# Making the summed weights of layer 1's Strassen-like units in DRAM, ahead of their use

## The chip, the cores and the metric

The kernel runs on one core of a Trainium2 chip. The metric is the device time of one execution in microseconds (us), lower is better. A measurement is a set of runs; the middle one counts.

## What is computed

Two decoder layers on one sequence of 512 tokens and 1024 channels, all in float32. Layer 0 is a Conformer convolution module followed by a SwiGLU FFN, layer 1 is windowed attention over a shared key and value followed by a SwiGLU FFN, and a final RMSNorm closes. The change concerns the FFN of layer 1:

```
def swiglu_ffn(x, w_up, w_down):
    gate, up = jnp.split(x @ w_up, 2, axis=-1)
    return (jax.nn.silu(gate) * up) @ w_down
...
        h = h + swiglu_ffn(rmsnorm(h, norm_ffn[l]), ffn_w_up[l], ffn_w_down[l])
```

Here `w_up` is 1024 x 5632 and `w_down` is 2816 x 1024.

## The kernel before

**Chunks.** All weights lie in one DRAM tensor `W` as chunks of 128 x 1024 floats (512 KB). `PLAN` lists the chunks in the order in which TensorE uses them. For every chunk `advance()` is called once, as its matmuls are about to be written. It calls `load(u)`, which keeps the loads ahead of the use, and then splits up to three chunks ahead (L275): ScalarE (ACT) casts the raw chunk to the high part `whi` (L272), VectorE (DVE) subtracts to get the low part `wlo` (L275). Each product is then three matmuls, high x high, high x low, low x high (L354 to L356 in `mm3`, L846 for layer 1's down projection). There are four buffers each for `raw`, `whi` and `wlo`.

**The engines' queues.** Each engine works through its instructions in order. SyncE (SP) issues the plain loads. GpSimd (POOL) issues the adding DMAs, and a DMA that has to wait keeps what stands behind it on POOL waiting too. Plain and adding DMAs are queues q1 and q0 of the profile; both run on the same 16 DMA engines.

**Order of the work.** Convolution; layer 0's FFN in two parts, `HALVES0`: pairs 0 to 4 (once for each half of the tokens), then pairs 5 to 10 for all tokens, the "second part" (`ffn_part(0, 1, ...)`, 24 up chunks and 12 down chunks); key and value (4 chunks); queries (8 chunks) with attention interleaved; output projection (8 chunks); then layer 1's FFN by `STEPS1`, and the output.

**Layer 1's units.** Six of eleven up pairs (`SEVENS`) and five steps of the down projection (`low`) are done with seven products in place of eight, in the manner of Strassen and Winograd: 11 units of seven chunks each. Four of a unit's seven weight blocks are not plain blocks but sums, with the blocks A11 to A22 of the weight matrix:

```
SUMS = {"S1": ("A21", "A22"), "S2": ("A11", "S1"), "S3": ("A21", "A11"), "S4": ("A12", "S2")}
```

The signs are in the right-hand blocks, so that all four are additions. S2 needs S1, and S4 needs S2.

**How a sum is made before.** `load(u)` has three loops. The first runs up to nine chunks ahead and loads a sum's first block from `W` into a `sum` tile in SBUF (four buffers, L252, SP). The second loads plain chunks into `raw`, up to six ahead (L258, SP). The third, up to six ahead, issues the adding DMA for the second block (L264, POOL): from `W` for S1 and S3, from the `sum` tile of S1 or S2 for S2 and S4. Nothing of this begins before attention's buffers are given back, since the tiles come from a pool that is opened then. There are 44 sums: 44 loads of first blocks and 44 adds, 22 from `W` and 22 from another `sum` tile.

**Others that the prediction names.** In layer 0's second part `evac` multiplies gate and up on POOL (L642), and ACT splits the product (L516). In attention POOL scales the probabilities (L1320) ahead of the transposes on TensorE. In layer 1 a unit's evacuation combines the seven products on DVE and POOL (L789 to L806, with L792 on POOL and L798 on DVE), L820 makes the sums of the right-hand side, and L764 evacuates a plain pair; L855 and L853 add the down projection into the residual.

Of the kernel before, what the change touches and what calls it, by code (L numbers as in the profile page):

```python
# [11 lines left out]
F32 = mybir.dt.float32  # L12
F32R = mybir.dt.float32r
AF = mybir.ActivationFunctionType
ALU = mybir.AluOpType
# [3 lines left out]
P = 128  # L19
D = 1024  # L20
S = 512
# [54 lines left out]
SUMS = {"S1": ("A21", "A22"), "S2": ("A11", "S1"), "S3": ("A21", "A11"), "S4": ("A12", "S2")}  # L76
# [6 lines left out]
def is_block(c):  # L83
    return isinstance(c[2], str) if len(c) == 3 else False


def chunk_plan():
    plan = []

    def pw2():  # L90
        for g in range(2):
            for kp in range(KT // 2):
                plan.append(("pw2", kp, g))

    def ffn(layer, lo, hi):
        for pair in range(lo, hi):
            plan.extend(ups(layer, pair))
        for g in range(2):
            for kp in range(lo, hi):
                plan.append(("down", layer, kp, g))  # L100

    for _ in range(2):
        pw2()
        ffn(0, *HALVES0[0])
    ffn(0, *HALVES0[1])
    for part in range(2):
        for half in range(2):
            plan.append(("kv", part, half))
    for quarter in range(4):
        for half in range(2):  # L110
            plan.append(("q", half, quarter))
    for part in range(2):
        for g in range(2):
            for kp in range(2):
                plan.append(("o", part * 2 + kp, g))
    for kind, pair in STEPS1:
        plan.extend(blocks_of(kind, pair) if kind == "low" or by_seven(1, pair) else ups(1, pair))
    for g in range(2):
        plan.append(("down", 1, LAST, g))
    return plan  # L120


PLAN = chunk_plan()
# [5 lines left out]
CHUNK_AT = {c: i for i, c in enumerate(CHUNKS)}  # L129
# [70 lines left out]
def hybrid_trunk(ctx: ExitStack, tc: tile.TileContext, xT, W, prm_in, wdw_in, sinks, relb, onehot, fin, lead, out):  # L200
    nc = tc.nc
    cpool = ctx.enter_context(tc.tile_pool(name="const", bufs=1))
    quads = ctx.enter_context(tc.tile_pool(name="quads", bufs=11))
    wpool = ctx.enter_context(tc.tile_pool(name="wts", bufs=4))
# [3 lines left out]
    dpool = ctx.enter_context(tc.tile_pool(name="dram", bufs=1, space=DRAM))  # L208
# [3 lines left out]
    def uid(s):  # L212
        ctr[0] += 1
        return f"{s}{ctr[0]}"
# [4 lines left out]
    def quad(dt=F32R):  # L219
        return quads.tile([P, 4, 512], dt, tag="quad", name=uid("quad"))  # L220
# [6 lines left out]

    stream = {"dma": 0, "split": 0, "use": 0}
    raws, splits = {}, {}
    DMA_AHEAD, SUM_AHEAD, SPLIT_AHEAD = 6, 6, 3  # L230
    BASE_AHEAD = 9
    stream.update(base=0, sum=0)
    lo_engine = [nc.vector]
    biased = [None]
    sums_pool = [None]
    latest = []
    sums = {}

    def is_sum(c):
        return is_block(c) and c[2][0] == "S"  # L240

    def chunk(c, name=None):
        return W[CHUNK_AT[c if name is None else c[:2] + (name,)]]

    def load(u):
        while stream["base"] < min(len(PLAN), u + BASE_AHEAD):
            c = PLAN[stream["base"]]
            if is_sum(c):
                if sums_pool[0] is None:
                    break  # L250
                sums[c[2]] = raws[stream["base"]] = t = sums_pool[0].tile([P, 1024], F32, tag="sum", name=uid("sum"), bufs=4)
                nc.sync.dma_start(t, chunk(c, SUMS[c[2]][0]))  # L252
            stream["base"] += 1
        while stream["dma"] < min(len(PLAN), u + DMA_AHEAD):
            i = stream["dma"]
            if not is_sum(PLAN[i]):
                raws[i] = r = wpool.tile([P, 1024], F32, tag="raw", name=uid("raw"), bufs=4)
                nc.sync.dma_start(r, chunk(PLAN[i]))  # L258
            stream["dma"] += 1
        while stream["sum"] < min(stream["base"], u + SUM_AHEAD):  # L260
            c = PLAN[stream["sum"]]
            if is_sum(c):
                add = SUMS[c[2]][1]
                nc.gpsimd.dma_start(raws[stream["sum"]], made[c[:2] + (add,)] if add[0] == "S" else chunk(c, add),  # L264
                                    accum_op=ALU.add)
                made[c] = raws[stream["sum"]]
            stream["sum"] += 1

    made = {}

    def split_weights(hi, lo, src):
        on_act = nc.scalar.copy(hi, src).ins  # L272

        with tc.issue_after(biased[0]) if biased[0] else nullcontext():
            latest[:] = [on_act, lo_engine[0].tensor_sub(lo, src, f32(hi)).ins]  # L275

    def advance():
        u = stream["use"]
        load(u)
        while stream["split"] < min(len(PLAN), u + SPLIT_AHEAD):  # L280
            i = stream["split"]
            stream["split"] += 1
            if i in NATIVE:
                splits[i] = (raws.pop(i), None)
                continue
            hi = wpool.tile([P, 1024], F32R, tag="whi", name=uid("whi"))
            lo = wpool.tile([P, 1024], F32R, tag="wlo", name=uid("wlo"))
            splits[i] = (hi, lo)
            split_weights(hi, lo, raws.pop(i))
# [418 lines left out]
    class Rows:  # L708
# [12 lines left out]
        def sums(self):  # L721
            f = [quad(F32) for _ in range(2)]
            for i in range(KT):
                nc.scalar.mul(f[i // 4][:, i % 4, :], h[i], col(self.gain, i))
            b11, b12, b21, b22 = (x[:, :, s] for x in f for s in HALF)
            t1 = self.pool.tile([P, 1024], F32, tag="sum", name=uid("t1"), bufs=4).rearrange("p (k s) -> p k s", k=4)

            for name, t, f, a, b in (("T1", t1, nc.gpsimd.tensor_sub, b11, b12), ("T3", b12, nc.gpsimd.tensor_sub, b22, b12),
                                     ("T2", b11, nc.gpsimd.tensor_add, b12, b11), ("T4", b21, nc.gpsimd.tensor_sub, b11, b21)):
                f(t, a, b)  # L730
                yield
                both = quads.tile([P, 2, 4, 256], F32R, tag="quad", name=uid("rows"))
                self.block[name] = [both[:, a] for a in range(2)]
                split(self.block[name], t, name == "T2")
# [129 lines left out]
    raw = [x[:, HALF[1]] for x in xg]  # L864
# [13 lines left out]
    with tc.tile_pool(name="conv", bufs=2) as cv:  # L878
# [299 lines left out]
        base = seen[0]  # L1178
# [22 lines left out]
    base = seen[0]  # L1201
# [12 lines left out]
    nxt = Next(("kv", "mix1"))  # L1214


    if True:
        ffn_part(0, 1, x0["ffn0"], ALL, Both(), nxt.on_h)
        x, rms = nxt.x, nxt.rms
# [153 lines left out]
        def step():  # L1373
            next(pipe, None)
# [5 lines left out]
        for part in range(2):  # L1380
            for g in range(2):
                def heads_of(kt):
                    return tuple(os_[part, kt // 2][:, 2 * a + kt % 2, :] for a in range(2))

                if part == 0:

                    ws = [get("o", kp, g) for kp in range(2)]
                    banks = {}
                    for m0, kp in ((0, 0), (0, 1), (2, 0), (2, 1)) if g else ((0, 0), (2, 0), (0, 1), (2, 1)):
                        order = [(k, m) for k in range(2) for m in (m0, m0 + 1)]  # L1390
                        if kp:
                            order = [(k, m) for m in (m0, m0 + 1) for k in range(2)]
                        for k, m in order:
                            if m not in banks:
                                banks[m] = bank()
                            mm3(banks[m], [w[:, k, m * P:(m + 1) * P] for w in ws[kp]], heads_of(2 * kp + k),
                                kp == 0 and k == 0, kp == 1 and k == 1)
                            if kp and k:
                                nc.vector.tensor_add(h[g * 4 + m], banks[m], h[g * 4 + m])
                        if (g, m0, kp) in ((0, 0, 1), (1, 0, 0), (1, 2, 0), (1, 2, 1)):  # L1400
                            step()
                    continue
                banks = [bank() for _ in range(4)]
                down_group([(("o", part * 2 + kp, g), 2 * kp) for kp in range(2)], heads_of, banks)
                for m in range(4):
                    i = g * 4 + m
                    nc.vector.tensor_add(h[i], banks[m], h[i])
                    nxt.on_h(i)
            if part == 0:
                drain(pipe)  # L1410
                attn.close()
                seven = ExitStack()
                pool7 = sums_pool[0] = seven.enter_context(tc.tile_pool(name="seven", bufs=2))
                nxt = Rows("ffn1", pool7)

    flips = iter([(t, g) for t in range(NBLK) for g in range(2)])
# [9 lines left out]
    for kind, pair in STEPS1:  # L1426
# [6 lines left out]
        if by_seven(1, pair):  # L1433
            c = seven_pair(pair, nxt, pool7, flip if pair == SEVENS[0] else None)
        else:
            c = plain_pair(pair, nxt, pool7)
# [68 lines left out]
```

## Time and profile before

| | us |
|---|---|
| median of 3 runs | 1078.13 |
| lowest, highest run | 1073.57, 1079.31 |
| the profiled execution, its own time | 1076.19 |
| its span, first to last instruction | 1074.4 |

| engine | busy, share of the span |
|---|---|
| TensorE (PE) | 98% |
| VectorE (DVE) | 70% |
| ScalarE (ACT) | 51% |
| GpSimd (POOL) | 40% |

A busy time counts an instruction from start to end. Matmuls overlap, so a busy TensorE is not one at its peak; what can be read is where it is idle. A row of a timeline gives start and duration in us, the engine, the line and the tiles, and in brackets the idle time before it and what ended it. A row of a waits view gives the sum of such waits in us, their number and the longest. In the DMA view a queue has its packets, the MB moved, and the share of the stretch in which its packets kept the 16 DMA engines.

### The profile page before, as it was taken

What the parts mean: (1) busy time and instruction counts of PE and PEld (TensorE: products, weight loads), DVE (VectorE), ACT (ScalarE), POOL (GpSimd) and SP (SyncE); (2) the same over time, 40 slices, a digit from 0 to 9 for tenths busy, and PEclk for the clock granted to TensorE, in tenths of its full rate; (3) what the DMA queues carried; (4) which work ended last, traced back from release to release, by engine and by line L of the source; (5) the groups of instructions that cost most, each with busy time, mean ns of one, the idle gap of its engine ahead of it and who ended that gap; (6) DMA issues with size and microseconds to landing.
All of it is one profiled execution on the core that took longest, in us unless ns stands there. A gap on an engine that the chain in (4) does not pass through costs nothing.

```text
span 1074.4 us, 15965 instructions
## 1 busy us (share of the span) xinstructions
PE 1054.1 (98%) x5878; PEld 914.7 (85%) x5878; DVE 752.3 (70%) x1159; ACT 551.8 (51%) x968; POOL 428.6 (40%) x523
## 2 busy tenths in 40 slices
PE   9999999999999999999999999999999998999996
PEld 7888889999988888888888777788889897798885
DVE  3999987977777644434546566578776867859687
ACT  3887887765565333322343565475543444443453
POOL 3999997710321211111111354116433416425331
PEclk9999999999999999999999999999999999999998
DMA  9238045565565432223323211375689698888932
GB/s 353 87 97 98 3 153 201 176 227 187 177 186 186 158 98 98 99 98 98 97 79 99 79 59 60 126 187 129 186 213 240 193 275 226 235 211 244 242 99 79
DMA packets 50651, 164.86 MB, mean 153 GB/s; under 512 B 5483, under 2 KB 11788, under 8 KB 50572
## 3 DMA queue, kind: packets, MB, share of 16 engines
q1 hardware_dynamic: 43516, 139.67, 40.2%
q0 software_dynamic: 6336, 23.07, 11.6%
q10 hardware_dynamic: 720, 1.10, 0.3%
q8 instruction: 46, 0.75, 0.3%
q14 instruction: 33, 0.27, 0.1%
HBM read 147.04 MB, written 5.24 MB: 142 GB/s over the span
## 4 chain that ended last, share of the span: by engine, by line
PE 86%; DMA 6%; DVE 5%; issue 2%; POOL 1%; ACT 0%; SPq 0%; POOLq 0%; DVEq 0%; ACTq 0%
PE bank L354 18%; PE bank L356 18%; PE bank L355 17%; PE bank L904 10%; PE bank L386 5%; PE bank L846 5%; PE bank L352 4%; DMA sum<-sum 4%; PE bank L387 3%; DMA sum<-in_W_dram 2%; DVE wlo L275 2%; PE bank L1301 1%; PE bank L1343 1%; PE bank L1330 1%; DVE h L855 1%
## 5 line engine op out<-in xcount | busy, mean ns | idle before, releaser
L356 PE MATMUL bank<-quad,wlo 128*128 128x512 f32 (+1 forms) x1008 | 348.7, 346 | 2.2 <-DVE wlo L275 2.2
L354 PE MATMUL bank<-quad,whi 128*128 128x512 f32 (+1 forms) x1008 | 349.1, 347 | 0.0
L355 PE MATMUL bank<-quad,whi 128*128 128x512 f32 (+1 forms) x1008 | 348.7, 346 | 0.0
L275 DVE TENSOR_TENSOR wlo<-raw,whi 128x1024 fp32r<-128x1024 f32 x175 | 241.8, 1383 | 151.3 <-ACT whi L272 150.7
L272 ACT CAST whi<-raw 128x1024 fp32r<-128x1024 f32 x175 | 183.2, 1048 | 217.3 <-PE bank L355 144.3
L356 PEld LDWEIGHTS bank<-quad,wlo 128*128 128x128 f32 x1008 | 190.9, 189 | 26.2 <-DVE wlo L275 2.6
L354 PEld LDWEIGHTS bank<-quad,whi 128*128 128x128 f32 x1008 | 190.9, 189 | 24.5 <-issue 1.6
L355 PEld LDWEIGHTS bank<-quad,whi 128*128 128x128 f32 x1008 | 190.9, 189 | 23.2 <-issue 0.2
L946 POOL TENSOR_TENSOR pr<-pr,pr 128x256 f32<-128x256 f32 x208 | 156.5, 785 | 8.0 <-ACT pr L945 7.9
L953 DVE SCALAR_TENSOR_TENSOR bank<-apad,wdw,bank 128x256 f32<-128x256 f32 x248 | 112.4, 484 | 3.4
L945 ACT ACTIVATE pr<-apad,wdw 128x256 f32<-128x256 f32 x208 | 98.4, 501 | 15.0 <-POOL pr L946 13.2
L904 PE MATMUL bank<-quad,w 128*128 128x256 f32 x448 | 98.7, 380 | 0.0
L904 PEld LDWEIGHTS bank<-quad,w 128*128 128x128 f32 x448 | 84.9, 190 | 11.8 <-issue 0.2
L275 DVE TENSOR_TENSOR wlo<-sum,whi 128x1024 fp32r<-128x1024 f32 x44 | 64.0, 1455 | 18.3 <-ACT whi L272 18.1
L272 ACT CAST whi<-sum 128x1024 fp32r<-128x1024 f32 x44 | 46.0, 1047 | 58.9 <-PE bank L355 18.9
L465 POOL TENSOR_TENSOR tmp<-tmp,tmp 128x256 f32<-128x256 f32 (+1 forms) x28 | 26.7, 955 | 123.3 <-ACT tmp L461 86.6
L386 PE MATMUL bank<-quad,whi 128*128 128x512 f32 x212 | 75.9, 398 | 0.0
L264 POOL DMA_DIRECT2D sum<-sum x22 | 19.3, 875 | 120.1 <-DMA sum<-in_W_dram 45.0
L642 POOL TENSOR_TENSOR tmp<-tmp,tmp 128x512 f32<-128x512 f32 x12 | 17.2, 1433 | 112.0 <-DVE tmp L641 112.0
L387 PE MATMUL bank<-quad,wlo 128*128 128x256 f32 x212 | 59.3, 280 | 0.0
L356 PE MATMUL bank<-rows,wlo 128*128 128x256 f32 x192 | 54.4, 284 | 3.5 <-DVE wlo L275 3.5
L846 PE MATMUL bank<-wlo,fhi 128*128 128x512 f32 x140 | 55.3, 395 | 1.9 <-DVE wlo L275 1.9
(222 smaller groups left out, 1703.5 us busy)
## 6 DMA issues: line engine op xcount, KB each, us to landing
raw<-in_W_dram SPq DMA_DIRECT2D x187, 512.0 KB, 3.8
sum<-in_W_dram SPq DMA_DIRECT2D x44, 512.0 KB, 5.4
sum<-in_W_dram POOLq DMA_DIRECT2D x22, 512.0 KB, 7.4
sum<-sum POOLq DMA_DIRECT2D x22, 512.0 KB, 7.1
w<-in_W_dram SPq DMA_DIRECT2D x14, 512.0 KB, 8.7
fd<-fs SPq DMA_DIRECT2D x1, 3072.0 KB, 34.3
h<-in_xT_dram SPq DMA_DIRECT2D x8, 256.0 KB, 8.4
bias<-fd SPq DMA_DIRECT2D x8, 256.0 KB, 5.1
```

The source lines that it names most:

```text
L272: on_act = nc.scalar.copy(hi, src).ins
L275: latest[:] = [on_act, lo_engine[0].tensor_sub(lo, src, f32(hi)).ins]
L354: nc.tensor.matmul(out, w[0], x[0], start=start, stop=False)
L355: nc.tensor.matmul(out, w[0], x[1], start=False, stop=False)
L356: nc.tensor.matmul(out, w[1], x[0], start=False, stop=stop)
L386: nc.tensor.matmul(first[2], first[0], first[1], start=start, stop=False)
L387: nc.tensor.matmul(second[2], second[0], second[1], start=False, stop=stop)
L846: nc.tensor.matmul(out, x, w[:, ws], start=first and e == 0 and i == 0, stop=e == 1 and i == 2, skip_group_check=True)
L904: mm = nc.tensor.matmul(self.pb[:, w * W2:(w + 1) * W2], w1_of(ct, w, k), x[k] if x else xg[k][:, tok], start=k == 0, stop=k == KT - 1)
L945: on_act = nc.scalar.mul(pr, a[:, j:j + W2], tap(j))
L946: on_pool = nc.gpsimd.tensor_add(pr, acc, pr)
L953: on_dve = nc.vector.scalar_tensor_tensor(yt if i == nd - 1 else c, src, tap(i), c if i else self.shift, op0=ALU.mult, op1=ALU.add)
```

## The change

The sums are no longer made in SBUF as they are needed. `prepare()` is a generator that is started ahead of layer 0's second part and moved on by one step in every call of `advance()`, ahead of the loads. A step issues, for one sum, a copy of its first block from `W` to a DRAM tile of its own (SP), and three steps later the adding DMA onto that tile (POOL), whose source is `W` for S1 and S3 and the DRAM tile of S1 or S2 for S2 and S4. The order of the sums puts S4 of the unit before between S1 and S2, and the adds take 47 steps: the second part's 36 chunks, key and value, and seven chunks of the queries. In layer 1 a sum is then loaded like any chunk, into one of the four `raw` buffers, six ahead. The `sum` tiles in SBUF and `load`'s first and third loop go; a scratch tile (`t1`) that shared their buffers keeps one. The adding DMA now bears a cap of 4096 bytes on a contiguous piece; the copy has none. What is computed is the same.

```
+    def load(upto):
+        while stream["dma"] < min(len(PLAN), upto):
             i = stream["dma"]
-            if not is_sum(PLAN[i]):
-                raws[i] = r = wpool.tile([P, 1024], F32, tag="raw", name=uid("raw"), bufs=4)
-                nc.sync.dma_start(r, chunk(PLAN[i]))
+            r = wpool.tile([P, 1024], F32, tag="raw", name=uid("raw"), bufs=4)
+            nc.sync.dma_start(r, chunk(PLAN[i]))
+            raws[i] = r
             stream["dma"] += 1
-        while stream["sum"] < min(stream["base"], u + SUM_AHEAD):
...
+    def prepare():
+
+        units = [c[:2] for c in PLAN if is_block(c) and c[2] == "S1"]
+        adds, todo, before = [], [], None
+        for u in units:
+            adds += [u + ("S1",), *([before + ("S4",)] if before else []), u + ("S2",), u + ("S3",)]
+            before = u
+        adds.append(before + ("S4",))
+        for c in adds + [None] * 3:
+            if c is not None:
+                summed[c] = dpool.tile([P, 1024], F32, tag=uid("sum"), name=uid("sum"))
+                nc.sync.dma_start(summed[c], chunk(c, SUMS[c[2]][0]))
+                todo.append(c)
+            if c is None or len(todo) > 3:
+                a = todo.pop(0)
+                nc.gpsimd.dma_start(summed[a], chunk(a, SUMS[a[2]][1]), accum_op=ALU.add, max_dma_last_dim=4096)
+            yield
...
     def advance():
         u = stream["use"]
-        load(u)
+        next(preparing[0], None)
+        load(u + DMA_AHEAD)
...
+    preparing[0] = prepare()
     if True:
         ffn_part(0, 1, x0["ffn0"], ALL, Both(), nxt.on_h)
```

More of the change, by code (lines that the diff above doesn't have):

```diff
@@ L229, in hybrid_trunk @@
     raws, splits = {}, {}
-    DMA_AHEAD, SUM_AHEAD, SPLIT_AHEAD = 6, 6, 3
-    BASE_AHEAD = 9
-    stream.update(base=0, sum=0)
+    DMA_AHEAD, SPLIT_AHEAD = 6, 3
     lo_engine = [nc.vector]
     biased = [None]
-    sums_pool = [None]
     latest = []
-    sums = {}
+    summed, preparing = {}, [iter(())]
     def is_sum(c):
@@ L242, in chunk @@
     def chunk(c, name=None):
[L243 to L254, printed above, removed]
+        if name is not None:
+            c = c[:2] + (name,)
@@ L255, in load @@
+        return summed[c] if is_sum(c) else W[CHUNK_AT[c]]
+    def load(upto):
+        while stream["dma"] < min(len(PLAN), upto):
             i = stream["dma"]
-            if not is_sum(PLAN[i]):
-                raws[i] = r = wpool.tile([P, 1024], F32, tag="raw", name=uid("raw"), bufs=4)
-                nc.sync.dma_start(r, chunk(PLAN[i]))
+            r = wpool.tile([P, 1024], F32, tag="raw", name=uid("raw"), bufs=4)
+            nc.sync.dma_start(r, chunk(PLAN[i]))
+            raws[i] = r
@@ L259, in load @@
             stream["dma"] += 1
-        while stream["sum"] < min(stream["base"], u + SUM_AHEAD):
[L261 to L269, printed above, removed]
+    def prepare():
[14 more added lines that the diff above has]
+            yield
@@ L725, in sums @@
             b11, b12, b21, b22 = (x[:, :, s] for x in f for s in HALF)
-            t1 = self.pool.tile([P, 1024], F32, tag="sum", name=uid("t1"), bufs=4).rearrange("p (k s) -> p k s", k=4)
+            t1 = self.pool.tile([P, 1024], F32, tag="sum", name=uid("t1"), bufs=1).rearrange("p (k s) -> p k s", k=4)
             for name, t, f, a, b in (("T1", t1, nc.gpsimd.tensor_sub, b11, b12), ("T3", b12, nc.gpsimd.tensor_sub, b22, b12),
@@ L1412, in hybrid_trunk @@
                 seven = ExitStack()
-                pool7 = sums_pool[0] = seven.enter_context(tc.tile_pool(name="seven", bufs=2))
+                pool7 = seven.enter_context(tc.tile_pool(name="seven", bufs=2))
                 nxt = Rows("ffn1", pool7)
```

## The prediction

> **What bounds the kernel now.** I read the page first: its busy times, its 40 slices, its chain of work that ended last.
>
> ```profile
> PE 1054.1 (98%) x5878; PEld 914.7 (85%) x5878; DVE 752.3 (70%) x1159; ACT 551.8 (51%) x968; POOL 428.6 (40%) x523
> ...
> DMA  9238045565565432223323211375689698888932
> ...
> PE 86%; DMA 6%; DVE 5%; issue 2%; POOL 1%; ACT 0%; SPq 0%; POOLq 0%; DVEq 0%; ACTq 0%
> ```
>
> TensorE is the bound, and 6% of the chain are transfers. The slices say where: from slice 15 (375 us) to slice 25 the DMA engines are at 2 to 3 tenths, in layer 1 (slices 27 to 37) at 6 to 9. The change moves transfers from the second stretch to the first. So I asked for the stages.
>
> ```profile
> core 0: us, PE busy (x) PEld busy (x) DVE busy (x) ACT busy (x) POOL busy (x), PEclk, DMA share, GB/s
> 0.00:25.00 25.00, 22.90 (x100) 19.81 (x101) 8.72 (x22) 7.24 (x17) 8.58 (x31) 1.00 0.93 349
> 375.00:575.00 200.00, 200.00 (x906) 166.53 (x905) 94.79 (x98) 66.43 (x84) 29.72 (x20) 1.00 0.29 95
> 575.00:700.00 125.00, 125.00 (x752) 98.53 (x752) 71.66 (x204) 60.85 (x171) 38.36 (x79) 1.00 0.26 86
> 730.00:785.00 55.00, 54.10 (x333) 48.30 (x332) 43.93 (x40) 29.84 (x40) 26.33 (x21) 1.00 0.64 173
> 785.00:875.00 90.00, 90.00 (x524) 79.79 (x523) 69.55 (x72) 41.51 (x50) 34.21 (x32) 1.00 0.84 221
> 875.00:925.00 50.00, 44.61 (x303) 40.50 (x303) 39.68 (x40) 22.00 (x27) 27.18 (x25) 1.00 0.88 245
> 925.00:980.00 55.00, 55.00 (x323) 48.85 (x322) 36.61 (x41) 22.77 (x28) 17.96 (x18) 1.00 0.83 218
> 980.00:1025.00 45.00, 42.82 (x267) 38.44 (x266) 34.42 (x35) 18.15 (x22) 19.66 (x18) 1.00 0.94 261
> ```
>
> In layer 1 TensorE is idle for 50.00 - 44.61 = 5.4 us in one stage, 45.00 - 42.82 = 2.2 us in another, and 0.9 us at the start. The largest hole, engine by engine (timelines of POOL, DVE, PE):
>
> ```profile
> 888.08 0.89 POOL L264 DMA_DIRECT2D sum<-sum  x1 [6.94 <-DMA sum<-sum]
> 888.69 1.61 POOL L792 TENSOR_TENSOR up<-up 128x512 f32<-128x512 f32 x1
> ```
> ```profile
> 890.33 0.69 DVE L798 TENSOR_TENSOR up<-up,bank 128x512 f32<-128x512 f32 x1 [6.61 <-POOL up L792]
> ...
> 892.03 3.43 DVE L275 TENSOR_TENSOR wlo<-sum,whi 128x1024 fp32r<-128x1024 f32 x1
> ```
> ```profile
> 895.51 0.39 PE L356 MATMUL bank<-rows,wlo 128*128 128x256 f32 x1 [3.50 <-DVE wlo L275]
> ```
>
> POOL waits 6.94 us for one adding DMA before it may issue the next, which adds that sum to another; its L792 stands behind, DVE's L798 waits 6.61 us for L792, the split of the next weights (L275) stands behind that, and TensorE starves for 3.50 us. POOL's waits over 700 to 1025 us say that this is a habit:
>
> ```profile
> POOL sum L264 <- DMA sum<-in_W_dram: 59.2, 14, 7.9
> ...
> POOL sum L264 <- DMA sum<-sum: 30.2, 5, 7.2
> ```
>
> **What the change takes away.** All 44 adding issues leave layer 1 (22 of each form, page), and with them these 89.4 us of POOL waits and the 0.88 us of each issue.
>
> ```profile
> L275 DVE TENSOR_TENSOR wlo<-raw,whi 128x1024 fp32r<-128x1024 f32 x175 | 241.8, 1383 | 151.3 <-ACT whi L272 150.7
> L272 ACT CAST whi<-raw 128x1024 fp32r<-128x1024 f32 x175 | 183.2, 1048 | 217.3 <-PE bank L355 144.3
> ...
> L264 POOL DMA_DIRECT2D sum<-sum x22 | 19.3, 875 | 120.1 <-DMA sum<-in_W_dram 45.0
> ```
>
> The sums come as plain chunks, so a hole needs a late load and no longer a late chain of load, add, add. I count the two holes as gone: 5.4 + 2.2 = **7.6 us**. The 0.9 us at the start I leave: that hole ends with an evacuation of the first plain pair (chain, in order of time), no sum.
>
> ```profile
> 742.80 0.61 DVE tmp L764
> 743.45 0.38 PE bank L354
> ```
>
> What is late next would be DVE: 39.7 of 50 us busy in the worst stage, so it has room on the mean, with no wait on POOL's DMAs in front of it.
>
> Layer 1 then loads through four raw buffers where four raw and four sum buffers stood. Cost: nothing, covered by time. In 785 to 875 us 28 loads were issued (rows below), 3.2 us each; four buffers last 12.9 us, of which a landing (5.6 us at today's traffic), a cast (1.05) and a subtraction (1.38) take 8.0. A load would have to be another 4.9 us late before each of the 11 units paid for it.
>
> **What it adds.** In the 47 chunks from the start of layer 0's second part: 44 copies from DRAM to DRAM (SP), 44 adds onto DRAM (POOL), 512 KB each, between the raw loads. No row shows either, so I bound them. The DMA view, in the order 375 to 575, 785 to 875 and 1062 to 1075 us:
>
> ```profile
> q1 hardware_dynamic: 5184, 18.88, 28.8%
> ...
> raw<-in_W_dram SPq DMA_DIRECT2D x37, 512.0 KB, 3.5
> ```
> ```profile
> q1 hardware_dynamic: 3604, 13.12, 43.4%
> q0 software_dynamic: 1834, 6.73, 40.4%
> ...
> raw<-in_W_dram SPq DMA_DIRECT2D x14, 512.0 KB, 5.6
> sum<-in_W_dram SPq DMA_DIRECT2D x14, 512.0 KB, 5.2
> sum<-in_W_dram POOLq DMA_DIRECT2D x7, 512.0 KB, 7.5
> sum<-sum POOLq DMA_DIRECT2D x6, 512.0 KB, 7.2
> ```
> ```profile
> q1 hardware_dynamic: 576, 1.05, 21.7%
> q10 hardware_dynamic: 576, 1.05, 21.7%
> ```
>
> - A load: with the queue full (0 to 25 us) 349 GB/s at a share of 0.93, so 0.524 MB take 0.524 / 375 GB/s = 1.40 us of all 16 engines.
> - An add into SBUF: 40.4% of 90 us for 6.73 MB, so 36.4 x 0.524 / 6.73 = 2.83 us, twice a load.
> - A store to DRAM: 43.4% of 13 us for 2.10 MB, so 1.41 us.
> - A **copy**: at least a load, 1.40 us, as it reads the same bytes; at most a load and a store one after the other, 2.81 us.
> - An **add onto DRAM**: at least 2.83 us; at most a store more, 4.24 us.
>
> The pair is between 4.23 and 7.05 us. For the low end speaks that adds from DRAM and from SBUF land alike (7.5 and 7.2 us), and that loads and stores take 1.4 us whichever side is DRAM. For the high end speaks that an add, which moves each byte twice on one side, costs double: a second pass is not hidden. No row has DRAM on both ends. I take the middle, **5.64 us**.
>
> The Trainium skill, page "DMA: Bandwidth & Descriptors", section "Latency and other measured facts", gives 214 GB/s per direction as the full rate of copies between HBM tensors: an estimate of 2.45 us for a copy here, and the only figure for it; no run here shows it. The Trainium skill, page "Collectives: The Full Stack", section "The bandwidth ceiling: the fold count and why AG ≠ RS ≠ AR", holds that a reduction takes double because of its two reads, which agrees with 2.83 against 1.40 us and would keep the add at 2.83. By these two pages of the Trainium skill the pair is 5.28 us, and the sum below moves to +13 us.
>
> **The sum.** A chunk takes 200 / 37 = 5.41 us of TensorE from 375 to 575 us. The first 40 steps (36 chunks of the FFN part, 4 of key and value) have that pace; after that attention stretches a chunk to 125 / 15 = 8.3 us (15 loads in 575 to 700 us) and everything fits. The engines need 1.40 + 4.23 = 5.63, 7.04 or 8.45 us for a chunk's load with a low, middle or high pair: over 40 chunks 9, 65 or 122 us more than TensorE. What absorbs it:
>
> ```profile
> 441.30 16.64 SPq L258 DMA_DIRECT2D raw<-in_W_dram  x4
> ```
> ```profile
> 444.40 1.05 ACT L272 CAST whi<-raw 128x1024 fp32r<-128x1024 f32 x1 [1.18 <-PE bank L355]
> ...
> 460.72 1.05 ACT L272 CAST whi<-raw 128x1024 fp32r<-128x1024 f32 x1 [4.39 <-PE bank L355]
> ```
>
> A load issued at 441.30 us lands 3.5 us later and is cast as the fourth from there, at 460.72: it may be 16 us late. And the adds may lie back: each is issued three steps behind its copy, SP runs some three chunks ahead of TensorE, and POOL's own work follows. I give that five adds of 2.83 us, 14 us; together 30 us. Left: 0, 35 or 92 us of starved TensorE. An estimate, by the middle: +35 - 7.6 = +27 us.
>
> The other parts cost nothing as far as rows say. POOL takes 44 issues of 0.88 us where it is busy 29.72 + 38.36 of 325 us. SP issues 44 copies and as many loads of sums as before; it mostly waits for a raw buffer:
>
> ```profile
> SPq L258 <- DVE wlo L275: 571.0, 150, 13.6
> ```
>
> Two waits are new. POOL's add waits for its copy, and the second sum's also for the first sum's add; behind it stand L642 and, in attention, L1320, and ACT's L516 waits for L642 with the casts L272 behind it. SP's load of a sum waits for its add, done long before.
>
> **Base.** The profiled execution took 1076.19 us, its span 1074.4 us; the median of the three runs, 1078.13, is 1.9 us above. 1076.2 + 27 = **1103 us**.
>
> **Rivals.**
> 1. *The engines have room; faster.* Price: -7.6 us and nothing back, **1069 us**. Decides: 30 us over 40 chunks is 0.75 us each, so a chunk may need 6.16 us and the pair 4.76 us. The low end, 4.23, is below that. For it: equal landing of both kinds of adds, and shares that count some waiting as work. Against it: only a fifth of the span between the bounds lies below 4.76.
> 2. *POOL's queue in attention; slower.* The engines keep up, but the adds wait at POOL's head as they do now: 89.4 us over 44, 2.0 us each. The 7 adds that stand among attention's POOL work delay L1320 and so the transposes, which TensorE takes in a fixed order: +14 - 7.6, **1083 us**. Against it: a copy is issued six chunks ahead of the point where TensorE needs POOL.
> 3. *Both cancel.* The pair is near 5 us, or layer 1's holes stay because DVE is the next bound there: **1076 us**, within 1073 to 1083.
>
> **Chances.** Forecast (engines full in layer 0, 1083 to 1130 us) 0.46; room 0.36; POOL 0.06; cancel 0.12. About 0.5%, 5.4 us, is what a measurement of this kernel can tell from no change. Faster 0.36, same 0.12, slower 0.52. Own range of the forecast: 1083 to 1130. The range must reach to the room case, 1064 (1069 less 4.6 us, by which the lowest run, 1073.57, lies below the median), and up to 1130; the upper bound itself, 1076 + 84 = 1160, is left out with about 0.1.
>
> **What will show it.** DMA slices from 375 to 600 us at 9 or more: engines full. TensorE holes there ending with DVE's wlo whose cast waited for a raw load, with landings of raw above 20 us: the forecast. The queues' shares over their bytes give the pair directly: above 4.76 us TensorE starves, below not. No TensorE hole from 875 to 1025 us: the 7.6 us are right. Waits of POOL L264 with L1320 behind: rival 2. I am wrong if a copy costs the engines what a load does.

## The result, and the profile after

| | us |
|---|---|
| before, median of 4 runs | 1078.72 (1073.57 to 1080.66) |
| after, median of 4 runs | 1175.23 (1173.88 to 1177.09) |
| ratio, 95% interval | 1.0904 (1.0863 to 1.0945) |
| the profiled execution of after: its own time, its span | 1173.88, 1172.1 |

The kernel became 9% slower, by 96.5 us; 1175 us lies above the predicted range, which ended at 1130. In the page of the kernel after, the busy times, the slices and the engines of the chain:

```profile
PE 1069.0 (91%) x5878; PEld 924.0 (79%) x5878; DVE 756.6 (65%) x1159; ACT 559.9 (48%) x968; POOL 436.1 (37%) x523
...
PE   9915574598999999999999999999999999999996
...
POOL 3462499988700322201101104340442323614221
PEclk9957786799999999999999999999999999999999
DMA  9999999945565566332323332122244536545641
...
PE 76%; issue 7%; DMA 6%; POOL 5%; DVE 3%; ACT 2%; SPq 0%; POOLq 0%; ACTq 0%
```

A slice is 29.3 us, counted here from 0. The hole in TensorE is at the wrong place for the forecast: slices 2 to 7, that is 60 to 230 us, the convolution. From slice 10 to the last but one, where the new transfers were expected, TensorE is at 9. The DMA engines are full in slices 0 to 7 and have room from 375 us on. The windows of before and of after over the same stretches (columns: stretch, its length, busy us of PE, PEld, DVE, ACT and POOL with their instructions, granted clock, share of the DMA engines, GB/s), before first:

```profile
25.00:125.00 100.00, 100.00 (x467) 87.00 (x466) 93.95 (x225) 80.64 (x181) 98.54 (x144) 1.00 0.42 84
125.00:225.00 100.00, 99.48 (x638) 92.78 (x637) 87.71 (x159) 79.71 (x159) 81.48 (x100) 1.00 0.48 159
```
```profile
25.00:125.00 100.00, 60.05 (x254) 50.17 (x253) 46.83 (x108) 27.71 (x63) 42.73 (x59) 0.78 1.02 303
125.00:225.00 100.00, 55.92 (x233) 45.83 (x231) 62.75 (x146) 57.53 (x120) 88.37 (x124) 0.78 1.06 229
225.00:375.00 150.00, 141.21 (x960) 133.93 (x960) 114.72 (x183) 103.22 (x194) 85.17 (x107) 0.95 0.57 174
375.00:575.00 200.00, 200.00 (x1036) 171.08 (x1035) 118.27 (x133) 86.20 (x128) 39.89 (x34) 1.00 0.46 142
```

Two things are to be seen. Before, POOL was busy for 98.54 of 100 us in the convolution: that stage has no room on POOL, and the prediction never looked at it. After, TensorE is idle there for 40 and 44 us of 100, and the clock granted to it falls to 0.78. In the first 100 us the other compute engines are less than half busy too, even POOL, which had no room there before; in the second POOL is at 88.37 again. Over the span TensorE is idle for 1172.1 - 1069.0 = 103.1 us, against 20.3 us before, and busy for 14.9 us more; together 97.7 us, the whole difference of the spans.

Why there? The view of the tile `sum` in the kernel after (L263 is the copy, L267 the add, L248 the load into SBUF; durations of the issues in ns, then the start of the first and of the last one in us):

```profile
L263 SPq DMA_DIRECT2D sum<-in_W_dram x44: 488/488/718, 31.4 to 112.1; - x44
L248 SPq DMA_DIRECT2D raw<-sum x44: 319/323/327, 814.2 to 1124.3; - x44
L267 POOL DMA_DIRECT2D sum<-in_W_dram x22: 812/818/1313, 36.2 to 155.8; - x22
L267 POOL DMA_DIRECT2D sum<-sum x22: 812/1378/3425, 138.6 to 216.2; - x22
```

The source starts `prepare()` ahead of layer 0's second part and moves it one step in each call of `advance()`. The chip saw something else: all 44 copies stand in SP's queue from 31.4 us, one behind the other, and all 44 adds stand in POOL's queue between 36.2 and 216.2 us. The kernel is built with `schedule_with_timeline_sim=True` (L1502): a scheduler lays each engine's instructions out by a simulated timeline, and an instruction with nothing to wait for may be put ahead of others that stand before it in the source. The copies read only the input `W` and write tiles of their own, so nothing held them. That this is the scheduler's reason is read from the code; the order itself is what the trace shows.

What POOL does with its 44 guests, from its waits over 25 to 300 us and its timeline around the longest hole of TensorE:

```profile
POOL sum L267 <- issue: 40.0, 10, 8.3
POOL sum L267 <- DMA sum<-in_W_dram: 22.7, 5, 7.2
```
```profile
76.77 0.81 POOL L267 DMA_DIRECT2D sum<-in_W_dram  x1 [4.53 <-DMA sum<-in_W_dram]
77.34 3.02 POOL L946 TENSOR_TENSOR pr<-pr,pr 128x256 f32<-128x256 f32 x4
82.82 0.81 POOL L267 DMA_DIRECT2D sum<-in_W_dram  x1 [2.46 <-issue]
83.38 0.99 POOL L957 TENSOR_TENSOR y<-y,pr 128x256 f32<-128x256 f32 x1
```
```profile
84.43 1.22 PE L973 MATMUL bank<-y,inv_s 128*128 128x256 f32 x2 [20.89 <-POOL y L957]
```

POOL waits 4.53 us for a copy before one add, does four of the convolution's products (L946), waits 2.46 us for the next add, and only then comes to L957, for which TensorE has been waiting 20.89 us. Over the whole span POOL waits 67.3 us before its 44 adds: the two rows above and 4.6 us for work of ACT. It is the chain that the prediction read in layer 1 (a waiting add, POOL's own work behind it, TensorE behind that), at another place. TensorE's waits over the whole span name the same engine first:

```profile
PE bank L973 <- POOL y L957: 33.3, 2, 20.9
PE bank L1002 <- DVE y L980: 19.2, 1, 19.2
PE bank L1002 <- POOL y L957: 17.5, 2, 15.3
PE bank L1002 <- ACT sq L982: 12.8, 1, 12.8
```

### The profile page after: what moved, and what is told of

Its sections match the earlier page's. It is cut to its first block, busy times and chain, and to the rows that moved or that the text cites. A ratio compares the mean times of both kernels' runs of the same rounds, so it can differ in the third digit from the quotient of the medians.

```text
span 1172.1 us, 16000 instructions
## 1 busy us (share of the span) xinstructions
PE 1069.0 (91%) x5878; PEld 924.0 (79%) x5878; DVE 756.6 (65%) x1159; ACT 559.9 (48%) x968; POOL 436.1 (37%) x523
## 4 chain that ended last, share of the span: by engine, by line
PE 76%; issue 7%; DMA 6%; POOL 5%; DVE 3%; ACT 2%; SPq 0%; POOLq 0%; ACTq 0%
PE bank L354 18%; PE bank L356 18%; PE bank L355 18%; PE bank L846 8%; PE bank L386 5%; POOL pr L946 4%; DMA sum<-in_W_dram 4%; PE bank L387 3%; DMA w<-in_W_dram 1%; DVE bank L953 1%; PE bank L352 1%; PE bank L1302 1%; PE bank L1344 1%; PE bank L1331 1%; DMA h<-in_xT_dram 1%
## 5 line engine op out<-in xcount | busy, mean ns | idle before, releaser
L274 DVE TENSOR_TENSOR wlo<-raw,whi 128x1024 fp32r<-128x1024 f32 x219 | 299.8, 1371 | 174.2 <-ACT whi L271 173.1
L271 ACT CAST whi<-raw 128x1024 fp32r<-128x1024 f32 x219 | 229.6, 1050 | 310.4 <-PE bank L355 208.6
L946 POOL TENSOR_TENSOR pr<-pr,pr 128x256 f32<-128x256 f32 x208 | 182.3, 1104 | 3.1 <-ACT pr L945 3.1
L945 ACT ACTIVATE pr<-apad,wdw 128x256 f32<-128x256 f32 x208 | 100.9, 504 | 115.2 <-POOL pr L946 107.4
L953 DVE SCALAR_TENSOR_TENSOR bank<-apad,wdw,bank 128x256 f32<-128x256 f32 x248 | 116.4, 486 | 17.3 <-PE bank L973 12.5
L904 PE MATMUL bank<-quad,w 128*128 128x256 f32 x448 | 103.0, 390 | 0.0
L904 PEld LDWEIGHTS bank<-quad,w 128*128 128x128 f32 x448 | 88.2, 197 | 13.4 <-issue 0.2
L820 POOL TENSOR_TENSOR up<-up 128x256 f32<-128x256 f32 x40 | 43.1, 1088 | 67.1 <-DVE up L766 65.3
L354 PE MATMUL bank<-rows,whi 128*128 128x256 f32 x192 | 54.6, 285 | 0.0
L355 PE MATMUL bank<-rows,whi 128*128 128x256 f32 x192 | 54.3, 283 | 0.0
```

What stands on the lines that cost most here:

```text
L354: nc.tensor.matmul(out, w[0], x[0], start=start, stop=False)
L355: nc.tensor.matmul(out, w[0], x[1], start=False, stop=False)
L904: mm = nc.tensor.matmul(self.pb[:, w * W2:(w + 1) * W2], w1_of(ct, w, k), x[k] if x else xg[k][:, tok], start=k == 0, stop=k == KT - 1)
L945: on_act = nc.scalar.mul(pr, a[:, j:j + W2], tap(j))
L946: on_pool = nc.gpsimd.tensor_add(pr, acc, pr)
L953: on_dve = nc.vector.scalar_tensor_tensor(yt if i == nd - 1 else c, src, tap(i), c if i else self.shift, op0=ALU.mult, op1=ALU.add)
```

## The experiments

Two theories stood first. "Place": the adds and copies cost what they cost because they run in the convolution, and moved to where the source has them they cost little. "Engines": the transfers cost about the same wherever they run, because the DMA engines are full. Line numbers shift by one or two in the experiments.

**e1_held** puts each copy into SP's queue behind the last raw load that the source issued, so that it can't be drawn ahead; the adds follow their copies.

```
-                nc.sync.dma_start(r, chunk(PLAN[i]))
+                last_load[0] = nc.sync.dma_start(r, chunk(PLAN[i])).ins
...
-                nc.sync.dma_start(summed[c], chunk(c, SUMS[c[2]][0]))
+                with tc.issue_after(last_load[0]):
+                    nc.sync.dma_start(summed[c], chunk(c, SUMS[c[2]][0]))
```

> Each copy is queued on SP behind the last raw load written ahead of it, so that copies, and with them the adds, run where the source puts them, from layer 0's second part on. Theory 'place' (the loss came from the copies and adds being issued between 31 and 216 us, in the convolution; the engines have room later: a copy costs 1.55 us and an add 2.7 to 3.1 us of the 16 engines in the changed kernel's trace, 4.3 to 4.7 us a pair): no hole in TensorE from 375 to 600 us, 1066 to 1072 us. Theory 'engines' (the forecast on record: the pair fills the 16 engines wherever it runs): about 1103 us, with holes from 375 to 600 us.

Measured: 1066.54 us, median of 4 (1064.47 to 1067.39), against 1078.8 of before; ratio 0.9883 (0.9856 to 0.991). The copies are issued from 354.9 to 584.2 us. Windows of e1_held:

```profile
25.00:125.00 100.00, 100.00 (x467) 87.00 (x466) 95.09 (x229) 80.24 (x181) 99.38 (x145) 1.00 0.42 82
375.00:475.00 100.00, 100.00 (x443) 82.79 (x442) 40.75 (x47) 30.14 (x39) 27.57 (x28) 1.00 1.02 293
475.00:575.00 100.00, 99.49 (x466) 83.39 (x465) 48.28 (x52) 36.13 (x48) 28.75 (x28) 1.00 1.01 286
875.00:925.00 50.00, 50.00 (x321) 45.59 (x320) 40.94 (x42) 22.86 (x28) 26.20 (x18) 1.00 0.58 179
980.00:1025.00 45.00, 45.00 (x273) 40.38 (x273) 32.80 (x34) 20.84 (x26) 11.60 (x8) 1.00 0.53 168
```

The convolution is whole again; from 375 to 575 us the DMA engines are full (shares of 1.02 and 1.01) and TensorE loses 0.5 us; both holes of layer 1 are gone. "Engines" falls, "place" stands, and this version is faster than both kernels. Its DMA view over 375 to 575 us gives the price that the prediction had to guess:

```profile
q0 software_dynamic: 5476, 19.94, 52.1%
q1 hardware_dynamic: 6336, 37.75, 49.1%
...
raw<-in_W_dram SPq DMA_DIRECT2D x36, 512.0 KB, 7.7
sum<-in_W_dram SPq DMA_DIRECT2D x36, 512.0 KB, 8.7
sum<-sum POOLq DMA_DIRECT2D x18, 512.0 KB, 8.7
```

q0 holds the adds: 52.1% of 200 us for 19.94 MB is 104.2 x 0.524 / 19.94 = 2.74 us each. q1 holds as many raw loads as copies: 98.2 x 0.524 / 37.75 = 1.36 us each on the mean of both. The pair is **4.10 us**. (Such a price is the time of a queue's packets, shared out over its bytes, and depends on what runs beside it; a price of copies almost alone stands under the next run.)

**e2_copies_early** leaves the copies where the scheduler puts them and orders only the adds, each behind the instruction that POOL got last from layer 0's FFN or from attention (one of four such places is shown).

```
-                nc.gpsimd.dma_start(summed[a], ..., accum_op=ALU.add, max_dma_last_dim=4096)
+                with tc.issue_after(on_pool[0]):
+                    on_pool[0] = nc.gpsimd.dma_start(summed[a], ..., accum_op=ALU.add, max_dma_last_dim=4096).ins
...
-                nc.gpsimd.tensor_mul(t2, t1, t2)
+                on_pool[0] = nc.gpsimd.tensor_mul(t2, t1, t2).ins
```

> The copies stay where the changed kernel has them (31 to 112 us); only the adds are queued on POOL behind its own work of layer 0's second part and attention. If POOL's queue was what the convolution lost (adds at its head, waiting), the copies do little: 1066 to 1080 us. If the full DMA engines were (late loads of weights and rows), a third to a half of the loss stays: 1100 us or more.

Measured: 1068.62 us in one run. The copies are issued from 32.1 to 96.7 us, the adds from 369.4 to 638.2 us. Windows of e2_copies_early, then the copies' queue over 32 to 112 us:

```profile
25.00:125.00 100.00, 100.00 (x466) 87.00 (x466) 94.22 (x225) 80.59 (x181) 98.54 (x145) 1.00 0.99 298
125.00:225.00 100.00, 97.91 (x614) 90.92 (x613) 85.70 (x156) 78.29 (x156) 79.53 (x97) 0.98 0.66 176
```
```profile
q1 hardware_dynamic: 2447, 25.05, 98.9%
```

In the first 100 us the DMA engines are as full as in the kernel after (0.99 against 1.02), and over both stretches TensorE loses 2 us instead of 84. So neither the copies' traffic nor their place in SP's queue hurts the convolution; it is the adds. Their transfers have left the convolution together with their issues (0.66 against 1.06 in the second stretch), so this run doesn't say which of the two it is; e7 and e8 below do. The queue's row gives 79.1 x 0.524 / 25.05 = 1.65 us a copy, with some small transfers counted in: more than the 1.36 us beside loads and adds, and with it the pair would be 4.39 us.

**e3_no_sums** makes no sums at all: no copies, no adds, and layer 1 loads the first block in the place of each sum (so the sums' second blocks are missing from the result).

```
-        return summed[c] if is_sum(c) else W[CHUNK_AT[c]]
+        return W[CHUNK_AT[c[:2] + (SUMS[c[2]][0],)]] if is_sum(c) else W[CHUNK_AT[c]]
...
-    preparing[0] = prepare()
```

> Leaves out all copies and adds; layer 1 loads the first block of each sum in the sum's place, so the output is not the reference's. This is the most that the change could bring. If layer 1's holes came from the sums (my step), 7.6 us less than before, 1068 to 1071 us. If DVE is the next bound there, the holes stay in part: 1073 to 1077 us.

Measured: 1064.79 us, median of 4 (1064.16 to 1064.91), ratio 0.9868 (0.9839 to 0.9897). This is the most that the change could bring, 14 us, some 3 to 6 us more than expected. Span against span it is 1074.4 - 1063.0 = 11.4 us: TensorE is idle for 8.5 us less (20.3 against 1063.0 - 1051.2 = 11.8) and busy for 2.9 us less. e1_held pays 1.7 us for making the sums.

**e4_two_copies** is e1_held with each copy issued twice, the second into a tile that nobody reads. It tells whether the engines' limit lies where the prediction's rule for it says.

> As e1_held, with every copy made twice (the second to a DRAM tile that nobody reads). By the sum on record, with 1.55 us a copy and 2.7 us an add, a chunk needs 1.40 + 3.1 + 2.7 = 7.2 us of the engines against 5.41 us of TensorE: 72 us over 40 chunks, less 30 us absorbed, so about 1110 us with holes. If the sum's rule is too strict, under 1080 us.

Measured: 1092.89 us in one run, 26.4 above e1_held. Windows, then rows of the DMA view over 375 to 575 us, of e4_two_copies:

```profile
475.00:575.00 100.00, 94.27 (x397) 74.39 (x395) 34.37 (x35) 25.16 (x32) 22.36 (x22) 0.98 1.04 326
575.00:700.00 125.00, 115.69 (x671) 92.29 (x671) 76.48 (x195) 63.18 (x164) 48.15 (x85) 0.96 0.73 222
```
```profile
q1 hardware_dynamic: 6459, 48.92, 62.8%
...
raw<-in_W_dram SPq DMA_DIRECT2D x31, 512.0 KB, 18.0
```

Now TensorE has holes and loads land after 18.0 us, where e1_held had 7.7. The expected figure was too high, as it was worked out from dearer transfers. With the measured prices a chunk needs 3 x 1.36 + 2.74 = 6.82 us of the engines against 5.41 us of TensorE: 40 x 1.41 = 56 us, less the 30 us that the prediction counted as absorbed, is 26 us. The number agrees, in one run, and partly by luck: the sum counted starved TensorE alone, but of the 28.1 us between the two spans only 15.1 are idle time of TensorE; in the other 13.0 it is busy (the clock granted in these stretches is 0.98 and 0.96). And of its waits from 375 to 730 us, 14.7 us, only 6.0 are for cast or split weights; 5.1 are for POOL. What the run does show is that on the far side of the limit loads land late and TensorE loses time. Its queue q1, with two copies to a load, takes 125.6 x 0.524 / 48.92 = 1.35 us for each of the three, as in e1_held with one: here a copy costs what a load does.

The next three took the place as it is in the kernel after and asked which part of an add costs POOL the time. **e5_ring** gives the queue of POOL's DMAs more room.

```
-    nc = bacc.Bacc("TRN2", target_bir_lowering=False, num_devices=1, dynamic_dma_scratch_size=2048)
+    nc = bacc.Bacc("TRN2", target_bir_lowering=False, num_devices=1, dynamic_dma_scratch_size=8192)
```

> As the changed kernel, with four times the room for the descriptors of POOL's DMAs (8192 in place of 2048 bytes of dynamic_dma_scratch_size); the instructions and their order stay. Theory 'ring' (from 80 to 150 us POOL stands before its adds, 40.0 us in the trace with no instruction to end the wait, because the adds issued before it have not drained and there is no room for more): those waits go, about 1135 us. Rival (POOL is held by the landing of the copies and by the adds' own issue time, whatever the room): 1165 us or more.

**e6_small_copies** cuts the copies into pieces of 4096 bytes, so that adds needn't wait behind large ones: `max_dma_last_dim=4096` on the copy of L263.

> As the changed kernel, with the copies cut into pieces of 4096 bytes where they have 32768. Theory 'turns' (queues take turns piece by piece, so a copy's 1.4 us piece against an add's 0.33 us piece leaves the adds 28% of the engines from 31 to 112 us, and they land after 44 us): adds land in under 20 us, POOL's waits shrink, 1100 to 1140 us. Rival (the engines' total work is what counts, not the turns): within 10 us of 1175.

**e7_thin_adds** adds only 64 of the 1024 columns (the other columns of a sum keep its first block): `summed[a][:, 0:64], chunk(...)[:, 0:64]` in L267 (the cap of 4096 bytes is left out; a piece has 256).

> As the changed kernel, but each add covers only the first 64 of 1024 columns, so the sums are mostly left out; 128 pieces of 256 bytes keep POOL's issue work and its places in the queue. If the convolution lost its time because the adds drain slowly (2.7 us of all engines each, behind the copies), little of the loss stays: 1075 to 1110 us, the rest being POOL's waits for the copies. If POOL's own issues and its waits for the copies are the loss, 1130 us or more.

Measured, one run each: e5_ring 1170.71, e6_small_copies 1182.24, e7_thin_adds 1155.67 us. The theories behind e5 and e6 fall; e7 came out on the side where POOL's issues and its waits for copies, not the adds' bytes, take most of the time. POOL's longest waits for an add over 25 to 300 us of e5_ring, of e6_small_copies and of e7_thin_adds:

```profile
POOL sum L267 <- DMA sum<-in_W_dram: 62.1, 15, 9.1
```
```profile
POOL sum L267 <- DMA sum<-in_W_dram: 72.6, 15, 9.3
```
```profile
POOL sum L267 <- issue: 32.8, 10, 6.3
POOL sum L267 <- DMA sum<-in_W_dram: 14.0, 4, 8.5
```

With the larger queue the 40.0 us of "issue" are gone, and 62.1 us of waiting for copies stand where 40.0 + 22.7 stood: one wait hid the other. Smaller pieces help nothing. Even adds of a sixteenth of the bytes keep 46.8 us of waits.

**e8_thin_both** thins the copies to 64 columns as well, and layer 1 loads the first block in a sum's place (the sums are not used). What is left is 44 issues on POOL, with almost nothing to move and little to wait for.

```
-            nc.sync.dma_start(r, chunk(PLAN[i]))
+            c = PLAN[i]
+            nc.sync.dma_start(r, W[CHUNK_AT[c[:2] + (SUMS[c[2]][0],)]] if is_sum(c) else chunk(c))
...
-                nc.sync.dma_start(summed[c], chunk(c, SUMS[c[2]][0]))
+                nc.sync.dma_start(summed[c][:, 0:64], chunk(c, SUMS[c[2]][0])[:, 0:64])
```

> Copies and adds at the changed kernel's places in the convolution, each over the first 64 of 1024 columns only; layer 1 loads the first block in a sum's place, so the output is not the reference's. What stays is POOL's issue work (44 issues) and hardly any transfer or wait for one. If POOL's waits for copies and drained adds were the loss, 1068 to 1085 us. If 44 issues of 0.8 us, and additions slowed beside them, among POOL's additions of the convolution (POOL busy 99% there) are enough, 1100 us or more.

Measured: 1112.94 us in one run, still 48 us above e3_no_sums, which issues none: the upper of the two expected cases. A window, TensorE's longest wait, POOL's waits for copies and two rows of POOL's timeline in e8_thin_both:

```profile
25.00:125.00 100.00, 63.07 (x268) 53.39 (x267) 57.23 (x134) 44.88 (x100) 88.54 (x121) 0.81 0.47 90
```
```profile
PE bank L476 <- POOL tmp L466: 25.7, 1, 25.7
```
```profile
POOL sum L268 <- DMA sum<-in_W_dram: 9.9, 3, 7.8
```
```profile
42.24 1.05 POOL L947 TENSOR_TENSOR pr<-pr,pr 128x256 f32<-128x256 f32 x1
42.91 4.66 POOL L268 DMA_DIRECT2D sum<-in_W_dram  x5
```

The DMA engines are at 0.47, near the 0.42 of before, and POOL is busy for 88.54 us, but with issues in place of its own work. The product of the first timeline row ends at 43.29 us, the five adds behind it at 47.57: 0.86 us each, close to the shortest issue in the kernel after, 0.81 us. So 44 issues are about 36 us, and the thin copies still cost POOL 9.9 us of waits; together 45.5 of the 48 us.

The same sum can be made for every version with the adds in the convolution: 44 x 0.81 us, plus POOL's waits before the adds over 25 to 300 us, against what the version lost to e3_no_sums (1064.8 us).

| us | waits before adds | with 44 issues | lost to e3_no_sums |
|---|---|---|---|
| after | 67.3 | 102.9 | 110.4 |
| e5_ring | 64.1 | 99.7 | 105.9 |
| e6_small_copies | 75.3 | 110.9 | 117.4 |
| e7_thin_adds | 52.1 | 87.7 | 90.9 |
| e8_thin_both | 9.9 | 45.5 | 48.1 |

It comes within 8 us of the loss in all five, which lie between 48 and 118 us. So POOL's time in the convolution accounts for nearly all of the loss; the few us that are left stay open. By the differences of the runs, after's 110.4 us come apart into 48.1 us (e8 less e3: issues, and waits for thin copies), 42.7 us (e7 less e8: POOL's waits for full-size copies) and 19.6 us (after less e7: what the adds' own full-size transfers add, 15.2 of it as longer waits of POOL). e5 to e8 are single runs, so this split is rough; that the adds' place in the convolution is the cause is shown by e1 and e2.

## Why the prediction was wrong, point by point

- **"Slower" came true by luck.** The forecast named full DMA engines in layer 0 and 1103 us. Nothing starves there in the kernel after, and with the work at the place that the forecast assumed the kernel is faster (e1_held).
- **Layer 1: right.** "I count the two holes as gone": from 700 us to the end TensorE has no wait in the kernel after, and the two windows of e1_held are full. The 7.6 us were a little short: TensorE's idle time falls by 8.5 us (the 0.9 us at the start goes as well) and its busy time by 2.9 us.
- **The step that failed: "In the 47 chunks from the start of layer 0's second part: 44 copies from DRAM to DRAM (SP), 44 adds onto DRAM (POOL), 512 KB each, between the raw loads."** They ran at 31 to 216 us. The prediction took the order of the source for the order on the engines. The sum was made against a stage with 29.72 of 200 us of POOL, and the work fell into one with 98.54 of 100. With the same work held at its place the kernel takes 1066.5 us, so the place alone costs 108.7 us, more than the whole slowdown.
- **"POOL takes 44 issues of 0.88 us where it is busy 29.72 + 38.36 of 325 us": right for that place,** as e1_held shows; at the real place the same 44 issues cost about 36 us, and their waits 67.3 us more.
- **The mis-sized term: "I take the middle, 5.64 us" for the pair.** Where the forecast had it run it is 4.10 us (e1_held), just below the low bound of 4.23, and 4.39 us with the dearest price of a copy. The add onto DRAM costs 2.74 us, no more than one into SBUF (2.83), and the copy about what a load does. "I am wrong if a copy costs the engines what a load does" was the right test. The Trainium skill, page "DMA: Bandwidth & Descriptors", section "Latency and other measured facts", has 214 GB/s per direction as the full rate of copies between HBM tensors, measured on tiles of 128 partitions with a padded row pitch, which gave the estimate of 2.45 us for a copy. The runs show 1.36 to 1.65 us, and the measurement decides. The Trainium skill, page "Collectives: The Full Stack", section "The bandwidth ceiling: the fold count and why AG ≠ RS ≠ AR", puts the double price of a reduction down to its two source reads. The factor agrees, 2.74 against 1.36 us; no trace here shows the reason.
- **The rule of the engines: right as far as two points show.** The pair decides at 4.76 us: on one side e1_held, at 4.10, loses 0.5 us of TensorE there; on the other e4_two_copies, with 4.10 + 1.36 = 5.46, is 26 us slower. The 30 us of absorption fit that, but part of the 26 us is no starvation, so they aren't measured.
- **Rival 1, "the engines have room", 1069 us,** is what happens when the work runs where the source puts it: 1066.5 us. Its reason holds too; only the place kept it from being the result.
- **Rival 2** had the right mechanism, adds that wait at POOL's head with TensorE's work behind them, at the wrong place. Where it put them it costs nothing: in e1_held POOL waits 141.0 us in 35 times for copies, and TensorE waits for none of it, since POOL has the time.

```profile
POOL sum L269 <- DMA sum<-in_W_dram: 141.0, 35, 9.8
```

- **A sign that was read wrongly:** full DMA engines from 375 us on were to mean starvation. In e1_held they are full and nothing starves. What tells is the landing of the loads, 7.7 us there against 18.0 in e4_two_copies; the prediction had this sign too, at 20 us.
- **Two small misreadings without effect:** the DMA digits of before from slice 15 to 25, counted from 1, go down to 1, not 2, and those of layer 1 down to 5, not 6.

Left open: why exactly an add waits for "issue" (the larger queue takes it away, so it has to do with room there, but no row names it), and whether the scheduler can be told of the place by other means than an order on the queue; neither was tried further.

## What to carry to other kernels

Where a scheduler orders the engines' queues, as here, work that waits for nothing may run long before the place where it is written: ask which engine has no room in every stage that it could be drawn into, and look at the first and last issue before anything else in the new trace. A DMA issued by a compute engine costs that engine its issue and its wait, and where that engine has no room (POOL, 98.54 of 100 us) nearly all of it is paid: 102.9 us of issues and waits, 110.4 us lost. Hold such work with an explicit order behind an instruction of the stage that has room: that turned 9% slower into 1.2% faster.

## What the runs showed of the hardware

- A copy from DRAM to DRAM takes the 16 DMA engines about as long as a load into SBUF: 1.36 us for 512 KB on the mean of both in e1_held, and 1.35 in e4_two_copies with two copies to a load. Almost alone, copies took 1.65 us (e2_copies_early); loads took 1.40 with the queue full and, by the same working, 57.6 x 0.524 / 18.88 = 1.60 us from 375 to 575 us in the kernel before.
- An add onto DRAM takes twice that, 2.74 us, like an add into SBUF (2.83 us).
- An add costs POOL about 0.8 us to issue, when nothing holds it up, and a product of the convolution that has its inputs mostly 0.69 us, with or without adds around it. The mean duration of the products seems to say otherwise. Their group in the page of before and of after (busy us, mean ns), a stretch of before, and two rows of after:

```profile
L946 POOL TENSOR_TENSOR pr<-pr,pr 128x256 f32<-128x256 f32 x208 | 156.5, 785 | 8.0 <-ACT pr L945 7.9
```
```profile
L946 POOL TENSOR_TENSOR pr<-pr,pr 128x256 f32<-128x256 f32 x208 | 182.3, 1104 | 3.1 <-ACT pr L945 3.1
```
```profile
L946 POOL TENSOR_TENSOR pr<-pr,pr 128x256 f32<-128x256 f32 x59 | 40.7, 727 | 0.0
```
```profile
84.07 0.99 POOL L946 TENSOR_TENSOR pr<-pr,pr 128x256 f32<-128x256 f32 x1
84.75 0.98 POOL L957 TENSOR_TENSOR y<-y,pr 128x256 f32<-128x256 f32 x1
```

  Behind an add a product's record is longer (0.99 us), but the next one starts 0.68 us after it, before it has ended. In the kernel before, 59 products from 30 to 75 us took 40.7 us, 0.69 each. So the records overlap, and the work goes on at the same pace: a mean of durations is no price where records overlap.
- The clock granted to TensorE was low where TensorE was idle: 0.78 in the two stretches with 40 and 44 us of 100 idle, and 1.00 from 375 to 575 us, without idle time.
